# Stick-breaking attention from running products and differences of v, with every step of the stage in a list written out ahead

## The chip, the core and the metric

The kernel runs on one core of one Trainium2 chip. A core has five engines with an instruction queue each: TensorE (PE in the profile; its weight loads are the row PEld), VectorE (DVE), ScalarE (ACT), GpSimd (POOL) and SyncE (SP), which here issues nearly all DMAs. Each engine works through its queue in order, and an instruction that needs another engine's result waits for a semaphore. The metric is the device time of one execution in microseconds (us); the time before is 2201.22 us, the median of three runs from 2200.82 to 2202.71 us.

## The reference, cut to what matters

The model is a trunk of two layers over 1024 tokens of width 1024, in float32: an RG-LRU layer and a SwiGLU feed-forward layer, then an attention layer and a second feed-forward layer, and a last normalisation. Only the attention is concerned. It has 16 heads of 64 and is causal, and it has no softmax:

```
z = einsum("bhqd,bhkd->bhqk", qb, kb) * scale
strict = s_idx < t_idx
log_fail = where(strict, log_sigmoid(-z), 0.0)
suffix = cumsum(log_fail, axis=3, reverse=True) - log_fail
weights = where(strict, exp(log_sigmoid(z) + suffix), 0.0)
out = einsum("bhqk,bhkd->bhqd", weights, vb)
```

With F(r) = sigmoid(-z(r)), the weight of key s for query t is sigmoid(z(s)) times the product of F(r) over all keys r with s < r < t. Call R(s) the running product of F from key t-1 down to key s, with R(t) = 1. Then the weight is also R(s+1) - R(s).

## The kernel before

Matrix products are computed in three passes: each operand is split into a rounded high part and a low part (type fp32r), and `mm3` (lines 267 to 270) issues high by high, high by low and low by high, each with 128 rows, 128 columns of weights and up to 512 moving columns. All weights are loaded raw (`load_raw`, line 249), rounded on ACT and subtracted on DVE.

The attention stage lies between the first feed-forward layer and the second. Heads are taken in eight pairs, q = 0 to 7. For a pair, `qkv_steps` (from line 1523) projects q, k and v: three kinds times two halves n of the tokens are six groups of eight steps, a step being one `mm3`. A group's result is scaled by the norm on DVE (line 1544), split on ACT and DVE (1553, 1554) and moved by SP (1555) into tiles in which both halves of the 128 partitions hold what one head needs. The v projection is turned by four transposes on PE (1569) and split again (1573, 1574).

The scores of one head are cut into 12 chunks. A chunk is a block of 128 queries j against up to 512 keys: eight chunks end at the diagonal (128, 256, 384 and 512 keys, for j modulo 4), four more take the first 512 keys of the later blocks. A chunk is two products (`z_part`, 1596 and 1597), and a diagonal chunk of 128 keys is computed over 256. Then `z_rest` follows: F = sigmoid(-z) on ACT (1616), w = sigmoid(z) on ACT (1617), a running product of F from right to left on DVE (1620 at the diagonal, 1622 for the others, which start from the value that the diagonal chunk ended with), and w times the shifted product on POOL (1623). POOL also clears a column (1608) and ACT copies one (1612).

The weights must be turned to be multiplied with v. A unit takes a block kb of 128 keys against the four query blocks of a half G: up to four transposes on PE (1634), a split on ACT and DVE (1643, 1644) and two products with v (1655, 1656). A head has four units for the first half of the queries and eight for the second; a pair has 24. After a head's last unit of a half, ACT and DVE add up its two parts (1665, 1666), and after the second head of the pair the result is split: for most pairs it goes to DRAM (1675 to 1678) and is brought back later by `bring_back` (1505, 1506), for the last it is written in place (1671, 1672).

The order is a loop over units, u from -8 on: one chunk's products, the transposes of unit u + 2, the rest of the chunk, one item of a list of small things to do, two steps of the filling work, the products of unit u. The filling work is the projection of the pair after. The last pair has no pair after it; there the filling work is the output product's first two results, o = 0 and 1, over seven of the eight pairs of heads (14 steps). PE, DVE, ACT and POOL follow this order as it is written (`tc.manual_schedule(engines={E.PE, E.Activation, E.DVE, E.Pool})`). SP isn't in that list: the framework places its DMAs, and it puts loads ahead of what stands before them in the program.

Before the loop, 32 steps project q and k of pair 0. The weights of the next kind are asked for at the beginning of the present one, and their splits stand in the list `later`.

After the attention, `mix_out_ffn_in` (from line 713) computes the 16 results of the output product, o = 0 to 15, four for each pair of rows j: d in (j, j + 4) and the token halves n. A result is 24 products, is added to the residual h on DVE (877), and feeds `v_steps`, which prepares the operands of the feed-forward layer. The first two results, begun earlier, are completed there with six products for pair 7. The residual's 16 tiles are loaded by SP (369) into space that tiles of the attention held.

The recurrent layer has its order from a planner already: the class `Plan` takes tasks with an engine, a duration, what must end before, and a rank, and emits them in the order in which they could begin, ties going to the lower rank.

Of the kernel before, what the change touches and what calls it, by code (L numbers as in the profile page):

```python
# [34 lines left out]
class Plan:  # L35
# [7 lines left out]
    def emit(self):  # L43
        left, end, free, table = set(range(len(self.tasks))), {}, dict(self.free), {}
        while left:
            best = None
            for i in left:
                eng, us, _, after, rank, tab = self.tasks[i]
                after[:] = [a if isinstance(a, int) else a[0][a[1]] for a in after]
                if any(a not in end for a in after):  # L50
                    continue
# [11 lines left out]
            if eng == "dma":  # L63
                free[eng], end[i] = begin + 0.5, begin + us
            left.remove(i)
            fn()


def lru_plan(plan, order, fn):
# [101 lines left out]
    for k in range(3):  # L171
        weights(f"out{k}")


@with_exitstack
def trunk(
# [305 lines left out]
    with ExitStack() as st:  # L482
# [153 lines left out]
        class Steps:  # L636
            def __getitem__(self, key):
                return lambda: acts[key[0]](*key[1:])

        with tc.manual_schedule(engines={E.PE, E.Activation, E.DVE, E.Pool}):  # L640
# [4 lines left out]
                Steps(),  # L645
# [67 lines left out]
    def mix_out_ffn_in(h, mix, bias, layer, gnext, ob):  # L713
# [13 lines left out]
        if begun:  # L727
            ps_.enter_context(pos)
        else:
            po = ps_.enter_context(tc.tile_pool(name="fpo", bufs=1, space=PSUM, reuse_waits="tile"))  # L730
            ob = po.tile([P, S], F32, name="ob")
# [109 lines left out]
        procs = {3: 3, 4: 4, 6: 5, 8: 6, 10: 7}  # L841
        with tc.manual_schedule(engines={E.PE, E.Activation, E.DVE, E.Pool}):
# [12 lines left out]
            for j in range(HK):  # L855
                rows = (j, j + HK)
                dn = [(d, n) for d in rows for n in range(NH)] if j else [(d, n) for n in range(NH) for d in rows]
                for k, (d, n) in enumerate(dn):
                    o = HK * j + k
                    if begun and o < 2:  # L860
                        ps = half(ob, o)
                        for i in range(2 if o == 0 else 0):
                            hi, lo = mix.w[rows[i]]
                            mm3(half(ob, i), hi[:, ND - 1], lo[:, ND - 1], xh[ND - 1][0], xl[ND - 1][0], False, True)
# [37 lines left out]
                    if sq_todo:  # L902
                        squares(h, *sq_todo.pop(0), rbc[1:], acc)
                if j == HK - 1:
# [576 lines left out]
    pos = ExitStack()  # L1481
    with ExitStack() as st:
        ap = st.enter_context(tc.tile_pool(name="ap", bufs=1))
        qs, mix = ExitStack(), [Mix(attn_w_o, 0)]
        psZ = st.enter_context(tc.tile_pool(name="psZ", bufs=2, space=PSUM, reuse_waits="tile"))
        psT = st.enter_context(tc.tile_pool(name="psT", bufs=2, space=PSUM, reuse_waits="tile"))
        psO = st.enter_context(tc.tile_pool(name="psO", bufs=2, space=PSUM, reuse_waits="tile"))
# [324 lines left out]
```

## Time and profile before

| what | value |
|---|---|
| median of three runs | 2201.22 us |
| profiled execution, its own time | 2203.1 us |
| span of its trace | 2201.3 us, 28255 instructions |
| mean granted TensorE clock | 0.995 |
| busy share over the span | PE 99%, DVE 78%, ACT 52%, POOL 10% |

The trace runs from the first to the last instruction; some 1.8 us of the profiled execution's time lie around it. A group's row gives the line, the engine, the operation, what is written and read, the shapes and a count; then the time in which the group was busy, the mean duration of one in ns, and the idle time of the engine just before them with what ended it. Products overlap in the pipeline: the duration of one is longer than the distance from its start to the next one's start, so PE counts as busy also in short waits. A row by stretches gives the stretch, its length, each engine's busy time with the instructions in brackets, the granted clock, the share of the DMA engines and GB/s.

### The profile page before, as it was taken

The numbers are of one execution on the slowest core, as the hardware profiler recorded it, in microseconds if no ns is written. First come the engines' busy times: TensorE is split into PE (matmuls) and PEld (weight loads), VectorE is DVE, ScalarE is ACT, GpSimd is POOL, SyncE is SP. The second block draws the span as 40 slices with busy tenths as digits, with TensorE's granted clock in tenths as the row PEclk, the third lists the DMA queues.
The fourth block names the chain that finished last, engine by engine and source line by source line (L and its number), as shares of the span: only waits on it lengthen the run. The fifth ranks groups of instructions, "written<-read, shape, count | busy, mean of one in ns | idle before, by whom it ended". The sixth has DMA issues, their size and how long they took to land.

```text
span 2201.3 us, 28255 instructions
## 1 busy us (share of the span) xinstructions
PE 2169.1 (99%) x10054; PEld 1799.9 (82%) x10054; DVE 1726.9 (78%) x2413; ACT 1146.2 (52%) x2041; POOL 225.3 (10%) x356
## 2 busy tenths in 40 slices
PE   9999999999999999999999999999999999999997
PEld 7888888888888888878888888778888888888886
DVE  7978678677777887968888888866876777788886
ACT  5577444444444554646666666653534444454455
POOL 0000010000000000003333334422000000000001
PEclk9999999999999999999999999999999999999999
DMA  4111312344444864452333333731133444466442
GB/s 173 39 48 48 124 39 91 98 139 139 151 144 133 283 198 128 130 147 75 99 90 93 97 104 88 216 110 48 57 116 117 151 137 151 149 236 225 136 136 86
DMA packets 132316, 273.50 MB, mean 124 GB/s; under 512 B 15312, under 2 KB 22608, under 8 KB 132176
## 3 DMA queue, kind: packets, MB, share of 16 engines
q1 hardware_dynamic: 131744, 270.92, 38.9%
q8 instruction: 79, 1.29, 0.2%
q10 hardware_dynamic: 432, 0.79, 0.1%
q14 instruction: 61, 0.50, 0.1%
HBM read 175.70 MB, written 70.78 MB: 112 GB/s over the span
## 4 chain that ended last, share of the span: by engine, by line
PE 87%; DVE 8%; ACT 3%; issue 1%; DMA 1%; SPq 0%; DVEq 0%; POOL 0%; ACTq 0%; POOLq 0%
PE p_ps L270 18%; PE p_ps L268 18%; PE p_ps L269 18%; PE a_ps L268 3%; PE a_ps L269 3%; PE a_ps L270 3%; PE qk_ps L270 3%; PE qk_ps L268 3%; PE qk_ps L269 3%; PE ob_ps L268 2%; PE ob_ps L269 2%; PE ob_ps L270 2%; PE wt_ps L1634 2%; DVE F L1622 2%; PE z_ps L1597 1%
## 5 line engine op out<-in xcount | busy, mean ns | idle before, releaser
L1623 POOL TENSOR_TENSOR w<-w,F 128x128 f32<-128x128 f32 (+1 forms) x192 | 185.8, 968 | 311.5 <-DVE F L1620 173.2
L268 PE MATMUL p_ps<-vh,wbh 128*128 128x512 f32 x524 | 204.7, 391 | 2.0 <-ACT ta L1183 2.0
L270 PE MATMUL p_ps<-vh,wbl 128*128 128x512 f32 x524 | 204.8, 391 | 0.0
L270 PE MATMUL p_ps<-vh,wcl 128*128 128x512 f32 x524 | 204.1, 390 | 0.5 <-DVE wcl L802 0.5
L269 PE MATMUL p_ps<-vl,wbh 128*128 128x512 f32 x524 | 204.3, 390 | 0.0
L270 PE MATMUL p_ps<-vh,wal 128*128 128x512 f32 x524 | 204.1, 389 | 0.1
L268 PE MATMUL p_ps<-vh,wch 128*128 128x512 f32 x524 | 204.1, 389 | 0.0
L269 PE MATMUL p_ps<-vl,wch 128*128 128x512 f32 x524 | 203.9, 389 | 0.0
L269 PE MATMUL p_ps<-vl,wah 128*128 128x512 f32 x524 | 203.9, 389 | 0.0
L268 PE MATMUL p_ps<-vh,wah 128*128 128x512 f32 x524 | 203.8, 389 | 0.0
L788 ACT CAST wbh<-sb 128x1024 fp32r<-128x1024 f32 (+2 forms) x69 | 69.6, 1009 | 192.5 <-DVE sb L772 192.5
L1620 DVE TENSOR_TENSOR_SCAN F<-F,unit 128x128 f32<-128x128 f32 (+3 forms) x128 | 128.2, 1002 | 5.7 <-ACT F L1616 5.7
L1643 ACT CAST th<-wt_ps 128x512 fp32r<-128x512 f32 x192 | 93.4, 487 | 68.9 <-PE wt_ps L1634 67.0
L1644 DVE TENSOR_TENSOR tl<-wt_ps,th 128x512 fp32r<-128x512 f32 x192 | 104.8, 547 | 25.4 <-ACT th L1643 24.1
L268 PE MATMUL qk_ps<-vh,whi 128*128 128x512 f32 x264 | 118.8, 450 | 0.7 <-ACT vh L348 0.7
L268 PEld LDWEIGHTS p_ps<-vh,wbh 128*128 128x128 f32 x524 | 98.6, 188 | 22.6 <-ACT ta L1183 2.5
L270 PEld LDWEIGHTS p_ps<-vh,wbl 128*128 128x128 f32 x524 | 98.7, 188 | 21.9 <-DVE wbl L792 1.3
L270 PEld LDWEIGHTS p_ps<-vh,wcl 128*128 128x128 f32 x524 | 98.4, 188 | 21.8 <-DVE wcl L802 1.4
L270 PEld LDWEIGHTS p_ps<-vh,wal 128*128 128x128 f32 x524 | 98.4, 188 | 21.4 <-DVE wal L783 1.0
L269 PEld LDWEIGHTS p_ps<-vl,wbh 128*128 128x128 f32 x524 | 98.7, 188 | 20.4
L269 PEld LDWEIGHTS p_ps<-vl,wch 128*128 128x128 f32 x524 | 98.4, 188 | 20.3
L269 PEld LDWEIGHTS p_ps<-vl,wah 128*128 128x128 f32 x524 | 98.4, 188 | 20.3
(403 smaller groups left out, 5695.9 us busy)
## 6 DMA issues: line engine op xcount, KB each, us to landing
raw<-in_ffn_w_in SPq DMA_DIRECT2D x88, 512.0 KB, 3.6
vl<-pd SPq DMA_DIRECT2D x128, 256.0 KB, 3.6
pd<-U SPq DMA_DIRECT2D x90, 256.0 KB, 2.3
raw<-in_ffn_w_out SPq DMA_DIRECT2D x28, 512.0 KB, 4.1
raw<-in_attn_w_qkv SPq DMA_DIRECT2D x24, 512.0 KB, 3.5
acc<-pd SPq DMA_DIRECT2D x28, 256.0 KB, 2.7
pph<-rbc SPq DMA_DIRECT2D x28, 256.0 KB, 2.5
ppl<-acc SPq DMA_DIRECT2D x28, 256.0 KB, 2.6
```

Source lines behind the costliest of these rows:

```text
L268: nc.tensor.matmul(ps, lhsT=wh, rhs=mh, start=first, stop=False, **kw)
L269: nc.tensor.matmul(ps, lhsT=wh, rhs=ml, start=False, stop=False, **kw)
L270: nc.tensor.matmul(ps, lhsT=wl, rhs=mh, start=False, stop=last, **kw)
L788: nc.scalar.copy(self.full(self.wb), self.full(self.sb))
L1597: nc.tensor.matmul(ps[:, 0 : c1 - c0], lhsT=lhsT, rhs=KL[q][hx][:, c0:c1], start=False, stop=True)
L1620: nc.vector.tensor_tensor_scan(rev, rev, unit[:, NB - n :][:, ::-1], first, op0=ALU.mult, op1=ALU.add)
L1622: nc.vector.tensor_tensor_scan(rev, rev, rev, first, op0=ALU.mult, op1=ALU.bypass)
L1623: nc.gpsimd.tensor_mul(wt, wt, F[:, 1 : n + 1])
L1634: nc.tensor.transpose(tp[:, c : c + P], W[q, hx, j, kb // 4][:, (kb % 4) * P : (kb % 4 + 1) * P], ident)
L1643: nc.scalar.copy(th[:, q0:], tp[:, q0:])
L1644: nc.vector.tensor_sub(tl[:, q0:], tp[:, q0:], f32(th)[:, q0:])
```

## The change

**Running products.** With R from above, the sum over s < t of (R(s+1) - R(s)) v(s) equals v(t) plus the sum over s up to t of R(s) (v(s-1) - v(s)), with v(-1) = 0. So the running product itself is turned and multiplied, with differences of v in place of v. The second sigmoid (1617), the product on POOL (1623), the cleared and copied columns (1608, 1612) go. New are a difference of v on DVE for each half and pair (`v_diff`), ahead of the transposes, and an addition of v to the result (`v_add`), also once for each half and pair. A diagonal chunk of 128 keys is now computed over 128 columns.

**One planned order.** `attention_plan` (new) enters all steps of the stage in a `Plan`, with durations and ranks: projections, splits, moves, chunks, units, sums, loads. SP is in the list of engines whose order is fixed. The 32 steps for q and k of pair 0 stand before the plan, written out; there a kind's weights are loaded, in SP's order, behind the moves of the groups before it.

**The last pair.** The chunks and units of pair 7 go by halves of the queries: the first half for both heads, then the second half for both.

**Output products.** Four results are computed in the attention stage, each over all eight pairs of heads: o = 0 and 1 of the first rows, copied on ACT into the tiles `rbc`, and the first two of the second rows, left in PSUM. Their weights are loaded and split in the plan; those of the second rows are loaded and split once more for their other token half.

The planner's loop is rewritten to look only at tasks that are ready, and the distance of two DMAs in it is 0.55 instead of 0.5. The diff, cut to its core:

```
+    def weights(i, name, r, raw, use):
+        ld = plan.add("dma", 2.6, fn["load", name], [raw], r - 4)
+        h0 = plan.add("act", 0.5, fn["whi", name, 0], [ld, use], r - 2.5)
+        l0 = plan.add("dve", 0.6, fn["wlo", name, 0], [h0], r - 2.3)
...
+            for x in range(4 + 4 * which):
+                src = (tl if x % 2 else th) if which == 0 else (tl if x // 2 % 2 else th)
+                old = [(zlast, q - 2)] if q > 1 else []
+                m = plan.add("dma", 2.1, fn["move", q, which, n, x], [src, m, *old], s + 0.4)
...
+            dv[q, n] = plan.add("dve", 0.66, fn["dv", q, n], [pt[i], before, turned], s + 0.4)
+            if q == NP - 1:
+                m = None
+                for y in range(NP - 1 - n):
+                    for x in range(2):
+                        m = plan.add("dma", 2.4, fn["back", y, n, x], [p, (kept, (y, n)), m], s + 0.5)
...
+    for c, (q, hx, j, ci) in enumerate(chunks):
+        s, dg = c - LEAD, j // 4 == ci
+        need = [sig.get(c - 2), moved.get((q, 0, j // 4, hx)), moved.get((q, 1, ci, hx))]
+        zlast[q] = zz = plan.add("pe", 2 * mm(n), fn["z", c], need, s)
...
+    for u, (q, hx, G, kb) in enumerate(units):
+        if u in turns:
+            turn[v] = t = plan.add("pe", 0.45, fn["vt", *v, len(ring)], [dv[v], *ring[-2:-1]], u - 1.9)
...
+        need = [scan[q, hx, j, kb // 4] for j in js] + ring[-2:-1]
+        T[u] = plan.add("pe", 0.109 * len(js) + 0.02, fn["T", u, len(ring)], need, u - 1.8)
...
+        vadd[q, G] = plan.add("dve", 0.66, fn["vadd", q, G], [g1, pt.get(6 * q + 4 + G)], s + 0.5)
...
+    for o in range(4):
+        for k in range(ND):
+            need = [p, bank, wlo[f"o{o}"][k // 4], back[k, 0] if k < NP - 1 else kept[NP - 1, 0]]
+            p = plan.add("pe", 0.685, fn["ob", o, k], need, s + 4 * o + k / 2 + 0.6)
...
-        procs = {3: 3, 4: 4, 6: 5, 8: 6, 10: 7}
+        procs = {2: 3, 3: 4, 6: 5, 8: 6, 10: 7} if begun else {3: 3, 4: 4, 6: 5, 8: 6, 10: 7}
...
+                    if begun and o < 2:
+                        ps = rbc[o]
+                    elif begun and o in (HK, HK + 1):
+                        ps = early[o - HK]
...
-            nc.scalar.activation(F[:, 0:n], ps[:, 0:n], AF.Sigmoid, scale=-SC)
-            nc.scalar.activation(wt, ps[:, 0:n], AF.Sigmoid, scale=SC)
...
-            nc.gpsimd.tensor_mul(wt, wt, F[:, 1 : n + 1])
...
-        with tc.manual_schedule(engines={E.PE, E.Activation, E.DVE, E.Pool}):
+        with tc.manual_schedule(engines={E.PE, E.Activation, E.DVE, E.Pool, E.SP}):
+            sts, later = stats_steps(), []
+            for i in range(4 * ND):
...
+                g, k = divmod(i, ND)
+                if k == 0:
+                    if g:
+                        was = (0, (g - 1) // 2, (g - 1) % 2)
+                        scaled(*was)
+                        q_hi(*was)
+                        q_lo(*was)
+                        for x in range(4 + 4 * was[1]):
+                            move(*was, x)
+                    if g % 2 == 0:
+                        name = (0, g // 2 + 1)
+                        load(name)
+                        later += [
...
+               project(0, g // 2, g % 2, k)
+               if i >= 5 and later:
+                   later.pop(0)()
+            plan = Plan(pe=0.0, dve=1.0, act=1.0, dma=1.0)
+            chunks, units = attention_plan(plan, Steps(acts))
+            plan.emit()
+            mix.load(2)
```

More of the change, by code (lines that the diff above doesn't have):

```diff
@@ L63, in emit, with __init__, __getitem__ @@
             if eng == "dma":
-                free[eng], end[i] = begin + 0.5, begin + us
-            left.remove(i)
-            fn()
+                free[eng], end[i] = begin + 0.55, begin + us
+            ready.remove(i)
+            for y in users[i]:
+                todo[y] -= 1
+                if todo[y] == 0:
+                    ready.append(y)
+            fn()
+class Steps:
+    def __init__(self, acts):
+        self.acts = acts
+    def __getitem__(self, key):
+        return lambda: self.acts[key[0]](*key[1:])
 def lru_plan(plan, order, fn):
@@ L1492, in trunk @@
+        unit = own([P, NB], "unit")
         nc.gpsimd.memset(unit[:, 0 : NB - P], 0.0)
         nc.gpsimd.tensor_copy(unit[:, NB - P :], ident)
[L1494 to L1506 removed]
```

583 lines of the change are left out of this document (351 added, 232 removed).

## The prediction

> **What bounds the kernel now.** I read the first page, then busy time by stretches of the attention, then one pair, then single waits.
>
> ```profile
> span 2201.3 us, 28255 instructions
> ...
> PE 2169.1 (99%) x10054; PEld 1799.9 (82%) x10054; DVE 1726.9 (78%) x2413; ACT 1146.2 (52%) x2041; POOL 225.3 (10%) x356
> ...
> PE 87%; DVE 8%; ACT 3%; issue 1%; DMA 1%; SPq 0%; DVEq 0%; POOL 0%; ACTq 0%; POOLq 0%
> ```
>
> TensorE is busy nearly all the time and carries 87% of the chain that ended last. The change takes almost nothing from TensorE, so removed work on ACT, or all of POOL's 225.3 us, is worth nothing by itself. What can be won is TensorE's waiting. Where it waits in the attention, by stretches: the last of q and k of pair 0; seven pairs with filling work; the rest of pair 7; the output product. The last row is one pair.
>
> ```profile
> core 0: us, PE busy (x) PEld busy (x) DVE busy (x) ACT busy (x) POOL busy (x), PEclk, DMA share, GB/s
> 960.90:980.80 19.90, 19.90 (x97) 16.94 (x96) 8.33 (x17) 4.39 (x7) 0.00 (x0) 0.97 0.49 130
> 980.80:1421.40 440.60, 435.34 (x2315) 365.90 (x2314) 385.96 (x533) 289.48 (x721) 171.67 (x294) 1.00 0.38 103
> 1421.40:1468.00 46.60, 38.07 (x200) 30.95 (x199) 37.93 (x49) 29.87 (x73) 18.87 (x25) 0.93 0.30 108
> 1468.00:1544.20 76.20, 76.20 (x338) 63.09 (x337) 48.74 (x58) 27.86 (x43) 13.36 (x10) 1.00 0.29 97
> ```
>
> ```profile
> 1165.90:1226.80 60.90, 60.17 (x323) 50.56 (x322) 53.80 (x75) 40.22 (x102) 23.59 (x40) 1.00 0.35 96
> ```
>
> Idle of TensorE: none at the beginning, 440.60 - 435.34 = 5.3 us over the seven pairs (60.90 - 60.17 = 0.73 in one), 46.60 - 38.07 = 8.5 us in the last, where the granted clock is also 0.93: another 0.07 x 46.6 = 3.3 us. So 5.3 + 8.5 + 3.3 = 17 us is what better order could win at most by these rows.
>
> **Removed and added work.** Rows of the attention, by shape:
>
> ```profile
> L1622 DVE TENSOR_TENSOR_SCAN F<-F,F 128x512 f32<-128x512 f32 x64 | 96.0, 1501 | 4.9 <-ACT F L1616 1.9 <-POOL w L1623 1.7 <-issue 0.3
> L1620 DVE TENSOR_TENSOR_SCAN F<-F,unit 128x128 f32<-128x128 f32 x32 | 30.4, 950 | 4.9 <-ACT F L1616 4.9
> L1676 DVE TENSOR_TENSOR oo<-oo,oh 128x512 fp32r<-128x512 f32 x13 | 8.7, 666 | 0.0
> ```
>
> ```profile
> 982.62 0.42 DVE L1620 TENSOR_TENSOR_SCAN F<-F,unit 128x128 f32<-128x128 f32 x1 [4.94 <-ACT F L1616]
> ```
>
> ```profile
> 1423.83 1.28 DVE L1622 TENSOR_TENSOR_SCAN F<-F,F 128x512 f32<-128x512 f32 x1 [0.24 <-POOL w L1623]
> ```
>
> On DVE a pair gets two differences and two additions of v, at 0.666 us from line 1676 (same size, two inputs): 4 x 0.67 = +2.7 us. The first 128-key scan, while POOL was still waiting for it, took 0.42 us against a mean of 0.95; the 512-key one above took 1.28 against 1.50. With POOL gone I take the short values: 4 x 0.53 + 8 x 0.22 = -3.9 us a pair. DVE goes from 53.8 to about 52.6 us of 60.9 and stays second; TensorE hides it. If the scans kept their means, DVE would have 56.5 us and still fit: neither value moves the sum.
>
> The Trainium skill, "SBUF — State Buffer", section "SBUF: two separate sides", says that a VectorE instruction with two SBUF inputs and a GpSimd instruction that reads SBUF lock each other out for a whole instruction. The two rows of the 128-key scan agree. By that rule alone the change should win what DVE loses to the lock; by the stretch of one pair it wins nothing there, since TensorE ends last.
>
> The diagonal chunk of 128 keys goes from 256 to 128 columns on TensorE. Starts of products one after another:
>
> ```profile
> 1167.42 0.22 PE L1655 MATMUL av_ps<-th,v 128*128 128x128 f32 x1
> 1167.48 0.27 PE L1656 MATMUL av_ps<-tl,v 128*128 128x128 f32 x1
> 1167.60 0.33 PE L1596 MATMUL z_ps<-kh,q 128*128 128x256 f32 x1
> 1168.52 0.36 PE L1597 MATMUL z_ps<-kl,q 128*128 128x256 f32 x1 [0.59 <-DMA kl<-ql__9921]
> ...
> 1171.01 0.28 PE L1596 MATMUL z_ps<-kh,q 128*128 128x256 f32 x1
> 1171.12 0.28 PE L1597 MATMUL z_ps<-kl,q 128*128 128x256 f32 x1
> 1171.24 0.60 PE L1634 MATMUL wt_ps<-ident,w 128*128 128x128 f32 x4
> ```
>
> Two of 256 columns take 1171.24 - 1171.01 = 0.23 us, two of 128 take 1167.60 - 1167.42 = 0.18. Four such chunks in a pair and eight pairs: 32 x 0.05 = **-1.6 us**.
>
> **The order in the seven pairs.** In the fence above the score product waits 0.59 us for a move of k. That is most of the 0.73 of the pair. The plan gives each group's moves one after another 2.1 us apart before a chunk may follow, though SP issues them 0.6 us apart (below), so this wait should go. Bounds: if new waits of the same size arise, 0; if all goes, the 5.3 us and no more. I take nearly all: **-5.0 us**. Late next would be the turned differences of v, see the rivals.
>
> **The last pair.**
>
> ```profile
> 1426.62 1.11 PE L1569 MATMUL vt_ps<-ident,t 128*128 128x128 f32 x4 [2.92 <-DVE t L1544]
> ...
> 1429.83 0.77 PE L268 MATMUL ob<-vh,whi 128*128 128x512 f32 x1 [2.10 <-issue]
> 1430.40 0.63 PE L269 MATMUL ob<-vl,whi 128*128 128x512 f32 x1
> 1430.83 0.63 PE L270 MATMUL ob<-vh,wlo 128*128 128x512 f32 x1
> ```
>
> TensorE waits here for v's last half and for output weights, and after that products start 0.57 and 0.43 us apart, not the 76.20 / 338 = 0.225 of the output stretch. The change gives this stretch 96 output products instead of the 42 of its two times seven steps; 54 x 0.225 = 12.2 us move here from the output stretch, TensorE's sum unchanged. The work without losses is 46.6 - 8.5 - 3.3 = 34.8 us, with the moved products 47.0 us. DVE has 37.9 us here and gets three more weight splits (two pieces each of 0.67) and the additions, about 43 us: less than 47, so the products can cover its chain. Bounds of what is won: 0 (they stand too late in the list) and 11.8 us (no loss left). I take nearer the upper one, as the row puts the waits at single places and the new list has 54 more products to set there: **-9.3 us**, 2.5 us staying lost.
>
> The cover of the end shrinks. Between the last unit and the first product that needs its result stood 6 + 21 products (6.1 us), now 21 (4.7 us), and an addition of 0.67 us joins the chain:
>
> ```profile
> 1467.32 0.39 PE L1656 MATMUL av_ps<-tl,v 128*128 128x512 f32 x1
> ...
> 1468.36 0.69 DVE L1666 TENSOR_TENSOR oo<-av_ps,oo 64x512 f32<-64x512 f32 x1 [1.23 <-ACT oo L1665]
> 1469.74 0.69 DVE L1672 TENSOR_TENSOR vl<-oo,vh 128x512 fp32r<-128x512 f32 x1 [0.69 <-ACT vh L1671]
> ```
>
> From 1467.32, the start of the last unit's second product, to 1469.74 + 0.69 = 1470.43 are 3.1 us, with the addition 3.9: still under 4.7, cost 0. Without the cover it would be 3.9 us, once.
>
> **The start of the stage.** Here the change adds a wait. SP's order becomes the written one, and there the load of the raw v weights of pair 0 stands behind the moves of q's second half. Before, the framework had loaded ahead; the first row below is that load:
>
> ```profile
> 946.12 0.33 SPq L249 DMA_DIRECT2D raw<-in_attn_w_qkv  x1
> ...
> 971.62 1.13 SPq L1555 DMA_DIRECT2D q<-qh__7630  x2
> 972.80 2.30 SPq L1555 DMA_DIRECT2D q<-ql__7631  x2
> 975.20 0.53 SPq L249 DMA_DIRECT2D raw<-in_attn_w_qkv  x1
> ```
>
> ```profile
> 972.24 1.28 DVE L1511 TENSOR_TENSOR wlo<-raw,whi 128x512 fp32r<-128x512 f32 x2
> 975.57 0.69 DVE L1544 TENSOR_TENSOR t<-qk_ps,rbc 128x512 f32<-128x512 f32 x1 [2.04 <-PE qk_ps L270]
> 976.99 0.69 DVE L1554 TENSOR_TENSOR ql__7678<-t,qh__7677 128x512 fp32r<-128x512 f32 x1 [0.73 <-ACT qh__7677 L1553]
> ```
>
> ```profile
> raw<-in_attn_w_qkv SPq DMA_DIRECT2D x24, 512.0 KB, 3.5
> ```
>
> ```profile
> 981.85 0.36 PE L1597 MATMUL z_ps<-kl,q 128*128 128x256 f32 x1 [0.76 <-DMA kl<-ql__7678]
> ```
>
> With the load at 975.2 instead of 946.12 the raw tile lands at 975.2 + 3.5 = 978.7; the split's first rounding takes about 0.65 on ACT, the two subtractions on DVE 1.28: 980.6. Behind them in DVE's queue stands the scaling of k's first half, which started at 975.57. It, the split, the moves and the score product shift by 980.6 - 975.57 = 5.0 us, to 986.9; the score product waits already, so all of it falls on TensorE, because the plan's first chunk has a lower rank (-8) than the v projection's first step (-7.5). Behind the wait come slow products as at 1429.83, about 1 us. **+6.0 us.** Bounds: 0, if the load is hoisted after all, and 5.0 + 3.3, if the clock costs what it cost in the last pair.
>
> The Trainium skill, "TensorE: Matmul & The Clock Gate", Part 1, says that the clock halves after an idle window of about 3.4 us and needs as long a busy one to return; the intervals after 1429.83 agree. By the page such a wait costs up to 1.7 us more, an estimate from 3.4 x 0.5, and the sum would be 0.7 us longer.
>
> Moved with no cost: output weights are loaded twice for two rows (2 loads, 4 roundings, 4 subtractions), hidden by the 47 us stretch. The planner's 0.55 doesn't reorder the recurrent layer, whose loads each wait for the one before.
>
> **The sum.** -1.6 - 5.0 - 9.3 + 6.0 = -9.9 us. The profiled execution took 2203.1 us (span 2201.3), which gives 2193.2; it stands 1.9 us above the median, so on the median's scale 2201.2 - 9.9 = **2191 us**.
>
> **Rivals.** *No wait at the start*: the load is placed early; 2191 - 6 = 2185. For it: the first recurrent stage fixed SP's order too, and TensorE has 99%. Against it: the diff writes the load behind the moves.
>
> *The last pair's gain stays out*: the plan sets the returns of stored results 2.4 us apart in a chain, so the products that need them stand late in TensorE's list, and the waits before them remain. 2191 + 9.3 = 2200. For it: up to 14 returns in the chain make 33 us of the 47. Against it: two results begin with the first return.
>
> *Behind the residual's loads.* SP issues them when tiles come free, and later weights stand behind them:
>
> ```profile
> 1467.75 7.84 SPq L369 DMA_DIRECT2D hh<-hd  x14
> 1475.96 0.33 SPq L249 DMA_DIRECT2D raw<-in_attn_w_o  x1
> ```
>
> If the fourth pair of weights now comes behind 16 loads (16/14 x 8.2 = 9.4 us, landing 3.5, splits 1.05 + 1.28) and these wait for the last addition (3.9), it is ready after 19 us; the products before it last 3 x 24 x 0.225 = 16.2. Cost about 3 us: 2194.
>
> *Slower: the turned differences of v.* They stand in the ring of transposes, and behind each stands every later unit. Their chain has one more DVE step than before, and in the fence of the last pair the old chain kept TensorE for 2.92 us. There are 14 turns under filling work. At 2.92 each the time is 2191 + 41 = 2232; from (2205.6 - 2191) / 14 = 1.05 us a turn on, the kernel is slower. Against it: the mean pair has only 0.73 us of waiting for two turns.
>
> **How the numbers follow.** My forecast 0.38 (2187 to 2196, its terms' middle values); no wait at the start 0.17; last pair's gain out 0.15; behind the residual's loads 0.10; slower by late turns, or by other waits that a fixed order adds, 0.20. 0.2% is 4.4 us, about what a measurement of this kernel can tell from no change. Faster by over that is below 2196.8: forecast, start and residual, 0.65. The last pair's 2200 is "same", 0.15. Slower 0.20. The lower end is 2177: no wait at the start and all 17 us won, taken 1.37 times, as the wait at 1168.52 cost 0.92 - 0.11 = 0.81 us where its row shows 0.59, since TensorE's overlap hides the rest: 2201.2 - 1.6 - 23. The upper end, 2208, is the slower case at 1.2 us a turn; beyond it lies about half of that case.
>
> **What would show it.** Right: DVE 40-odd of 47 us and TensorE over 44 of 47 in the last pair; an idle of some 5 us before the first score product with "DMA kl" as releaser; pairs of about 60 us; an output stretch of 64 us. Wrong: no such idle, or a pair longer than 61 us with waits on line 1569's successor or on transposes.

## The result, and the profile after

The changed kernel takes 2201.14 us (median of 12 runs, 2199.77 to 2202.80) where the kernel before, run beside it, takes 2202.68 us (12 runs, 2200.82 to 2206.23): a ratio of 0.9992, 95% interval 0.9984 to 1.0001. No difference can be told. The profiled execution took 2201.81 us, its span is 2200.0.

The first page of the changed kernel: busy time by engine, and the chain that ended last.

```profile
span 2200.0 us, 27262 instructions
...
PE 2167.9 (99%) x10054; PEld 1798.9 (82%) x10054; DVE 1709.1 (78%) x2434; ACT 1078.5 (49%) x1776; POOL 35.6 (2%) x44
...
PE 90%; DVE 5%; ACT 2%; DMA 2%; issue 1%; SPq 0%; DVEq 0%; ACTq 0%
```

993 instructions, 190 us of POOL's work and 68 us of ACT's are gone; TensorE's busy time differs by 1.2 us. DMA has gone from 1% of the chain to 2%. Medians here are of all executions, ratios and intervals of the fast ones alone: one of the six of moves_close was slow (2458.92 us, granted clock 0.831).

Busy time by stretches of the changed kernel: the seven pairs, the last pair, the output product.

```profile
core 0: us, PE busy (x) PEld busy (x) DVE busy (x) ACT busy (x) POOL busy (x), PEclk, DMA share, GB/s
988.30:1430.60 442.30, 434.60 (x2313) 365.64 (x2314) 366.66 (x548) 228.03 (x479) 0.59 (x6) 1.00 0.38 103
1430.60:1478.00 47.40, 46.15 (x248) 37.88 (x248) 35.37 (x53) 23.51 (x49) 0.00 (x0) 1.00 0.51 187
1478.00:1543.30 65.30, 65.30 (x289) 54.05 (x288) 51.35 (x59) 27.88 (x43) 13.63 (x10) 1.00 0.25 85
```

The last pair and the output product came out in size as forecast: 48 products more stand in the last pair, its stretch is as long as before, and the output stretch is 10.9 us shorter. The seven pairs still have 442.30 - 434.60 = 7.7 us without TensorE.

To compare kernels, the attention is cut below by four starts of products in each trace: the first product of q's projection, the 145th of the projections (before it lie the 144 products for q, k and v of pair 0, and the first chunks), the last of the projections, and the first of the output stretch, up to the first product of the feed-forward layer. What follows that lasts 655.6 to 657.9 us in every kernel. Start stretches of equal code differ by up to 4 us between traces; no reading of the start below hangs on less.

| kernel | start | seven pairs | last pair | output | median us |
|---|---|---|---|---|---|
| before | 47.3 | 423.6 | 46.9 | 76.2 | 2202.7 |
| after | 55.1 | 425.3 | 47.3 | 65.3 | 2201.1 |
| load_early | 47.3 | 427.3 | 47.2 | 65.3 | 2196.5 |
| moves_together | 54.3 | 418.3 | 47.3 | 65.3 | 2193.3 |
| moves_close | 56.3 | 420.5 | 47.2 | 65.3 | 2196.8 |
| both_edits | 45.0 | 417.5 | 47.3 | 65.3 | 2185.1 |
| load_on_pool | 45.1 | 418.7 | 47.3 | 65.3 | 2185.8 |
| both_and_pool_load | 45.0 | 417.8 | 47.3 | 65.3 | 2184.4 |
| pool_back | 52.1 | 438.4 | 48.2 | 65.3 | 2215.6 |
| both_pool | 47.6 | 424.5 | 48.3 | 65.3 | 2194.1 |
| two_results | 52.6 | 425.1 | 38.1 | 76.2 | 2203.7 |
| by_heads | 53.9 | 427.2 | 56.0 | 65.3 | 2210.8 |
| heads_two_results | 53.1 | 427.0 | 45.0 | 76.2 | 2211.8 |
| before_sp_fixed | 58.2 | 512.4 | 47.1 | 76.2 | 2302.8 |

The change won 10.4 us at the end (last pair and output), lost 7.8 at the start, and lost 1.7 in the seven pairs, where a gain of 6.6 had been forecast.

What TensorE waits for in the attention of the changed kernel (total, times, longest):

```profile
PE z_ps L1786 <- DMA kl<-ql: 8.3, 8, 1.6
PE z_ps L1786 <- DMA kh<-qh: 4.4, 1, 4.4
```

Nearly all of it is moves of k. The 4.4 us, and 0.62 of the 8.3, stand at the start. SP's, DVE's and TensorE's timelines there:

```profile
975.11 1.72 SPq L1746 DMA_DIRECT2D q<-ql  x1
976.87 0.58 SPq L425 DMA_DIRECT2D raw<-in_attn_w_qkv  x1
```

```profile
981.23 1.29 DVE L1701 TENSOR_TENSOR wlo<-raw,whi 128x512 fp32r<-128x512 f32 x2 [7.29 <-ACT whi L1697]
982.44 0.68 DVE L1723 TENSOR_TENSOR t<-qk_ps,rbc 128x512 f32<-128x512 f32 x1
```

```profile
987.01 0.44 PE L1786 MATMUL z_ps<-kh,q 128*128 128x128 f32 x1 [4.38 <-DMA kh<-qh]
988.07 0.44 PE L1786 MATMUL z_ps<-kl,q 128*128 128x128 f32 x1 [0.62 <-DMA kl<-ql]
988.31 0.74 PE L444 MATMUL qk_ps<-vh,whi 128*128 128x512 f32 x1
988.85 0.63 PE L445 MATMUL qk_ps<-vl,whi 128*128 128x512 f32 x1
989.28 0.63 PE L446 MATMUL qk_ps<-vh,wlo 128*128 128x512 f32 x1
```

This is the chain of the forecast: SP issued the raw load of v's weights at 976.87, behind the last move of q; its split on DVE ran from 981.23, and the scaling of k's first half started behind it, at 982.44. TensorE's wait is 4.38 + 0.62 = 5.0 us, and the products behind it start 0.54 and 0.43 us apart. By the view of stretches the granted clock (third number from the end) is 0.50 there:

```profile
988.30:991.50 3.20, 3.20 (x10) 2.63 (x11) 1.12 (x2) 0.79 (x2) 0.00 (x0) 0.50 0.82 185
```

The rest of the 8.3 us comes mostly once in each pair, at the 128-key chunk of the upper keys. One pair's wait on TensorE, and SP's timeline ahead of it:

```profile
1179.43 0.30 PE L1786 MATMUL z_ps<-kl,q 128*128 128x128 f32 x1 [1.09 <-DMA kl<-ql]
```

```profile
1172.36 1.11 SPq L1746 DMA_DIRECT2D kl<-ql  x2
1174.66 0.34 SPq L425 DMA_DIRECT2D raw<-in_attn_w_qkv  x1
1175.05 0.46 SPq L1746 DMA_DIRECT2D kl<-ql  x1
```

Three moves of k stand in the trace from 1172 to 1176, the last of them 0.39 us behind a 512 KB load. The time from issue to landing of these three (least, median, most):

```profile
DMA to landing us min/median/max: 2.5/2.5/4.3
```

The two ahead of the load land after 2.5 us. The one behind it takes 4.25: issued at 1175.05, landed at 1179.30, and the product that waits for it starts at 1179.43. The load itself was held in SP's list from 1173.52 to 1174.66, until DVE's split had freed its tile, and the moves behind it were held with it. Six pairs have this wait, 1.0 to 1.6 us long, and in the trace all six have the same picture: the move that ends the wait was issued 0.4 us behind a 512 KB load and landed after 4.2 to 4.8 us.

### The profile page after: what moved, and what is told of

The parts are those of the page before. It is cut to its first block, busy times and chain, and to the rows that moved or that the text cites. A ratio compares the mean times of both kernels' runs of the same rounds, so it can differ in the third digit from the quotient of the medians.

```text
span 2200.0 us, 27262 instructions
## 1 busy us (share of the span) xinstructions
PE 2167.9 (99%) x10054; PEld 1798.9 (82%) x10054; DVE 1709.1 (78%) x2434; ACT 1078.5 (49%) x1776; POOL 35.6 (2%) x44
## 4 chain that ended last, share of the span: by engine, by line
PE 90%; DVE 5%; ACT 2%; DMA 2%; issue 1%; SPq 0%; DVEq 0%; ACTq 0%
PE p_ps L446 18%; PE p_ps L444 18%; PE p_ps L445 18%; PE qk_ps L444 3%; PE qk_ps L445 3%; PE qk_ps L446 3%; PE z_ps L1786 3%; PE a_ps L445 3%; PE a_ps L444 3%; PE a_ps L446 3%; PE av_ps L1834 3%; PE wt_ps L1817 2%; PE ob_ps L444 2%; PE ob_ps L445 2%; PE ob_ps L446 2%; DMA kl<-ql 2%
## 5 line engine op out<-in xcount | busy, mean ns | idle before, releaser
L1798 ACT ACTIVATE F<-z_ps 128x512 f32<-128x512 f32 (+3 forms) x188 | 91.8, 490 | 168.3 <-PE z_ps L1786 167.2
L1805 DVE TENSOR_TENSOR_SCAN F<-F,unit 128x128 f32<-128x128 f32 (+3 forms) x128 | 104.8, 821 | 62.9 <-ACT F L1798 62.7
L444 PEld LDWEIGHTS p_ps<-vh,wah 128*128 128x128 f32 x524 | 98.4, 188 | 20.3
L444 PEld LDWEIGHTS p_ps<-vh,wch 128*128 128x128 f32 x524 | 98.4, 188 | 20.3
```

Of the source, the lines that this page charges most:

```text
L444: nc.tensor.matmul(ps, lhsT=wh, rhs=mh, start=first, stop=False, **kw)
L1798: nc.scalar.activation(F, Z.pop(c)[:, 0:n], AF.Sigmoid, scale=-SC)
L1805: V.tensor_tensor_scan(rev, rev, unit[:, NB - n :][:, ::-1], 0.0, op0=ALU.mult, op1=ALU.add)
```

## The experiments

My theory after this profile: two separate losses, both made by the new order of SP's list, eat the gain at the end. One is the load at the start, the other the place of the loads among the moves in the pairs. The rivals are with each run. Ratios are to the kernel before, run on the same chip.

**The start: the loads issued earlier (load_early).** Both raw loads that pair 0 still needs are issued with the first group.

```
                     if g % 2 == 0:
                         name = (0, g // 2 + 1)
-                        load(name)
...
+                    if g == 0:
+                        load((0, 1))
+                        load((0, 2))
```

> One edit on the changed kernel: the raw v weights of pair 0 are loaded beside those of k, at the first of the 32 written-out steps, ahead of all moves. Theory: the gap before the first score product (4.4 us in front of it and 0.6 us between its two halves, then slow products) is the late load alone; both waits shrink to under 1 us, and the time falls by 5.0 to 7.8 us, to about 2194 us. Rival (the gap comes from the written order of SP as a whole, or from the split and the moves of k, not from this load): the gap stays above 3 us and the time within 2 us of 2201.

2196.45 us, ratio 0.9970 (0.9958 to 0.9982): 4.7 us less than the changed kernel, a little short of the theory's 5.0 to 7.8. The start is 47.3 us again, as before the change: 7.8 us less. The first score product no longer waits for k. In the seven pairs 2.0 us more were lost; the waits on kl stay, 9.1 us. So the start's loss is the place of the load, and the pairs' loss is another one.

**The pairs: moves that don't hang on each other (moves_together, moves_close).** In the plan each move hung on the one before. The dependence is taken out; the time from a move to the chunk that needs it is set to 6.0 in one kernel and left at 2.1 in the other.

```
-                m = plan.add("dma", 2.1, fn["move", q, which, n, x], [src, m, *old], s + 0.4)
+                m = plan.add("dma", 6.0, fn["move", q, which, n, x], [src, *old], s + 0.4)
```

> One edit on the changed kernel: in the plan a move of q or k no longer follows the end of the move before it, and a move counts 6.0 us, so that the chunks stay about as late in TensorE's list as they are. The eight moves of a group then stand together in SP's list. Theory (loads, stores and the other half's moves stand between a group's moves and hold up the last one): TensorE's waits for kl, 8.3 us in all, fall under 2 us, and the time to about 2193 us (2191 to 2196). Rival (k's projection, scaling and split come late themselves): the waits stay, 2201 us.

> As the run with the moves together, but a move still counts 2.1 us in the plan, so that the first chunks of a pair stand some 4 us earlier in TensorE's list. Theory: the moves are together too, but a chunk may follow them so closely that four moves of 0.6 us and a landing of 2.3 us (4.7 us against 3.8 planned) are not done; half the gain, 2194 to 2200 us. Rival (order in TensorE's list does not matter): the same time as with 6.0 us.

With 6.0: 2193.29 us, ratio 0.9953 (0.9941 to 0.9965). With 2.1: 2196.77 us, 0.9965 (0.9953 to 0.9978). The seven pairs fall from 425.3 to 418.3 and 420.5 us. SP's list around the same pair with 6.0, and TensorE's waits on moves in the whole attention:

```profile
1166.94 1.29 SPq L1746 DMA_DIRECT2D kl<-ql  x2
1168.28 0.59 SPq L1746 DMA_DIRECT2D kh<-qh  x1
1168.91 1.24 SPq L1746 DMA_DIRECT2D kl<-ql  x2
1170.25 0.54 SPq L1895 DMA_DIRECT2D odh<-oh  x1
1171.21 0.33 SPq L425 DMA_DIRECT2D raw<-in_attn_w_qkv  x1
```

```profile
PE z_ps L1786 <- DMA kh<-qh: 4.7, 1, 4.7
PE z_ps L1786 <- DMA kl<-ql: 0.6, 1, 0.6
```

All the moves of the group now stand ahead of the store and the load. The waits on kl go from 8.3 to 0.6 us, and the 0.6 stands at the start; the 4.7 us ahead of the first score product stay, as that load wasn't touched. With 2.1, 5.3 us of waits on kl were left, in three waits, the longest 4.1. By the trace all three stand between 987 and 999 us, so they belong to the start; in the seven pairs no wait on a move is left with 2.1 either. The time lies in the forecast 2194 to 2200, but not for the reason given: no chunk of the pairs came too early for its moves. What the pairs lose against 6.0, 420.5 - 418.3 = 2.2 us, is in good part one wait near their end for v's split on DVE, 2.6 us instead of 1.5. What cured the pairs is that the moves no longer hang on each other; the planned time from move to chunk mattered little.

**Both (both_edits).**

> Both earlier edits in one kernel: the raw loads of the second and third kind of pair 0 are issued with the first group, and the plan's moves no longer hang on the move before. My theory (two separate losses, one at the start and one in the pairs): the gains add. The start's edit alone gave 0.30% against the kernel before and the moves' edit alone 0.47%, of which the last pair is common to both; beside the changed kernel (2201.1) they were 4.7 and 7.9 us, so 2201.1 - 12.6 = about 2188.5 us, ratio 0.993, no idle of over 2 us ahead of the first score product and under 1 us of waits on moves of k in all pairs. Rival (one loss seen in two places: whoever takes the first away finds the second later in the list): no better than the moves' edit alone, 2193, ratio 0.995 or more.

2185.11 us, ratio 0.9918 (0.9905 to 0.9932). The losses are separate: 0.22% and 0.39% against the changed kernel alone, 0.74% together, 0.13 more than their sum, about what one interval leaves open to either side. Start, pairs and end are now 45.0, 417.5 and 112.6 us against 47.3, 423.6 and 123.0 before.

**Is it the load in SP's list? (load_on_pool).** The same loads, at the same place in the program, are issued by POOL. Nothing else is changed.

```
-                raws[name] = load_raw(w_qkv[name[1] * ND + name[0]])
+                raws[name] = rp.tile([P, D], F32, tag="raw", name="raw")
+                nc.gpsimd.dma_start(raws[name], w_qkv[name[1] * ND + name[0]])
```

> The changed kernel with the 512 KB loads of the weights of q, k and v in the attention issued by POOL, which has almost nothing else to do there, instead of SP; their place in the written order stays. Theory (in SP's list the load waits for the tile's last reader and is then issued ahead of moves of k; the moves behind it are late for the wait and for the transfer ahead of them): the idle ahead of the first score product goes from 4.4 to under 1 us, as the load no longer stands behind the moves of q, and the waits on kl from 8.3 to under 3; 2201.1 - 4.7 - 6 = about 2190, ratio 0.994 to 0.996. Rival 1 (the transfers share the DMA engines whoever issues them): the start's idle goes, the waits on kl stay above 5 us, 2196. Rival 2 (issuing on POOL is slow, or the loads wait there for each other): new waits on weights, 2201 or more.

2185.81 us, ratio 0.9924 (0.9912 to 0.9936): this one edit brings what the two edits bring, 4 us more than I had expected. Start 45.1, pairs 418.7, waits on kl 1.5 us. In the same pair SP's and POOL's lists read:

```profile
1159.92 1.74 SPq L1747 DMA_DIRECT2D kl<-ql  x3
1161.70 1.24 SPq L1747 DMA_DIRECT2D kh<-qh  x2
1162.98 1.24 SPq L1747 DMA_DIRECT2D kl<-ql  x2
```

```profile
1162.81 0.54 POOL L1690 DMA_DIRECT2D raw<-in_attn_w_qkv  x1 [22.29 <-ACT th L1823]
```

POOL's queue, not SP's, now waits for the tile, and SP's moves go out without a pause. The moves of kl issued from 1158.6 to 1161.1 landed after 2.4 to 2.8 us. The move at 1162.98, 0.17 us behind POOL's load, took 4.9:

```profile
DMA to landing us min/median/max: 4.9/4.9/4.9
```

So rival 1 has a part of the truth: a 512 KB load slows the moves behind it, whichever queue issues it. No chunk was waiting for these. What cost time was that the load stood ahead of the urgent ones.

> Both edits together, and the attention's loads of weights of q, k and v issued by POOL. Theory (the remaining waits of the stage are not from SP's list: 0.2 us on moves of k were left): within 2 us of both edits alone, 2183 to 2187. Rival (the loads in SP's list still delay results' stores and moves that the profile's single waits don't show): 3 us or more faster, 2182 and below.

Both edits and the load on POOL: 2184.38 us, ratio 0.9916 (0.9902 to 0.9929), the fastest version run and within the error of both_edits. The remaining waits are not from SP's list.

**The order of SP alone, on the kernel before (before_sp_fixed).**

```
-        with tc.manual_schedule(engines={E.PE, E.Activation, E.DVE, E.Pool}):
+        with tc.manual_schedule(engines={E.PE, E.Activation, E.DVE, E.Pool, E.SP}):
```

> One edit on the kernel before: SP is added to the engines whose order is as written, nothing else. Theory: the raw v weights of pair 0 come behind q's moves as in the changed kernel, the first score product waits some 5 us more, and the kernel is 5 to 8 us slower than before (2207 to 2210 us); the pairs keep their period of 60.9 us, since in the written order a group's moves stand together. Rival (the fixed list costs nothing by itself): 2202 us.

2302.79 us, ratio 1.0448 (1.0435 to 1.0462). All expectations missed by far. Waits of TensorE, then of ACT (from 1000 to 1500 us):

```profile
PE z_ps L1596 <- ACT w L1617: 63.5, 25, 6.4
```

```profile
ACT whi L1510 <- DMA raw<-in_attn_w_qkv: 83.9, 13, 8.7
```

What the start lost on one load is lost here on many. In the order as it is written the raw loads stand behind moves, which wait for results; the rounding of the raw tile then stops ACT's queue, behind it wait the sigmoids of the chunks, and for these TensorE. In the kernel before, ACT has no such wait among its six largest from 1000 to 1420 us. The 63.5 us are not the whole loss of 100; the mean granted clock is also lower, 0.981. A fixed order of SP costs 100 us here as the program was written. The changed kernel's list costs some 16 us against the one of both_edits (2201.1 against 2185.1), which is fixed too: what costs is the order, not that it is fixed.

**POOL's work back (pool_back, both_pool).** For each chunk POOL multiplies the running products by themselves into a scratch tile, as dead work; first on the changed kernel, then on both_edits.

```
+            wd = own([P, 256], "wd", BF16)
+            for a in range(0, n, 256):
+                b = min(n, a + 256)
+                F = F_[q, hx, j, ci][:, a:b]
+                nc.gpsimd.tensor_mul(wd[:, 0 : b - a], F, F)
```

> The changed kernel with POOL's work beside the scans put back as dead work: for each chunk POOL multiplies the running products by themselves into a scratch tile of bf16 that nobody reads. Theory (the scans' time is worth nothing, as TensorE ends last): the 128-key scans go from 0.42 us back towards 0.95 and those of 512 keys from 1.22 to about 1.5, DVE's busy time rises by some 30 to 45 us, and the time stays within 3 us of the changed kernel's 2201. Rival (the change's gain in the pairs hangs on the scans without POOL beside them, and other losses ate it): 5 us or more slower, 2206 and up, with new waits of TensorE on transposes of the weights in the pairs.

2215.55 us, ratio 1.0060 (1.0046 to 1.0073): 14 us slower than the changed kernel, so the theory fell. But the rival's place was wrong too. Waits of TensorE from 960 to 1560 us:

```profile
PE z_ps L1786 <- DMA kl<-ql: 14.1, 7, 2.4
PE z_ps L1786 <- DMA kh<-qh: 3.7, 1, 3.7
PE vt_ps L1757 <- DVE dv L1751: 1.5, 3, 0.8
```

The waits on moves of k went from 8.3 to 14.1 us. In the pair shown above DVE's split frees the raw tile later: SP's load is held for 1.8 us instead of 1.1, the moves behind it come later, and the wait is 2.0 us instead of 1.09. So a slower DVE reached TensorE through SP's list. But that is at most 5.8 of the 13.1 us by which the seven pairs are longer (438.4 against 425.3). The dead product also does more than lengthen scans: it reads F, and ACT has to wait for it before it writes that tile again (waits of ACT from 990 to 1430 us; the changed kernel has none on POOL):

```profile
ACT F L1798 <- POOL wd L1812: 34.7, 25, 1.8
```

How much of the rest comes that way stays open.

> Both edits as in the earlier kernel that had them together, and POOL's dead product beside the scans put back. Theory (POOL's work costs only where a late VectorE step makes SP's load, and with it the moves behind it, late): with moves that do not hang on each other the same dead work costs little: 2185.1 + 0 to 4 = 2185 to 2189, waits on kl under 2 us. Rival (longer scans reach TensorE by another way, the weights' transposes or the turned differences of v): the same 13 to 15 us as on the changed kernel, 2198 to 2200.

2194.09 us, ratio 0.9958 (0.9944 to 0.9971): 9 us slower than both_edits, between theory and rival. With moves that no longer hang on the loads the waits on k are gone, and the next thing is late (waits from 990 to 1423 us):

```profile
PE vt_ps L1757 <- DVE dv L1751: 5.2, 9, 1.1
```

These are the turned differences of v. Seven of the nine waits, 4.0 of the 5.2 us by the trace, stand behind a difference that had itself waited for POOL, which clears the column ahead of v in its own queue, behind the dead products:

```profile
DVE dv L1751 <- POOL vt L1721: 3.0, 7, 0.9
```

In both_edits DVE never waits for POOL there. So the 9 us are not the price of longer scans alone, and these two runs don't say what the removal of POOL's work was worth in the change: they show that as much work on POOL, put there, costs 9 to 14 us. Scans by shape, both_pool and then both_edits:

```profile
L1807 DVE TENSOR_TENSOR_SCAN F<-F,F 128x512 f32<-128x512 f32 x56 | 78.6, 1403 | 9.2 <-ACT F L1798 9.0
...
L1805 DVE TENSOR_TENSOR_SCAN F<-F,unit 128x128 f32<-128x128 f32 x30 | 14.9, 495 | 0.2 <-ACT F L1798 0.2
```

```profile
L1807 DVE TENSOR_TENSOR_SCAN F<-F,F 128x512 f32<-128x512 f32 x56 | 71.6, 1279 | 12.3 <-ACT F L1798 11.9
...
L1805 DVE TENSOR_TENSOR_SCAN F<-F,unit 128x128 f32<-128x128 f32 x31 | 12.8, 414 | 0.2 <-ACT F L1798 0.2
```

The dead product adds some 0.1 us to the mean scan, less than the scans of the kernel before had lost (mean 0.95 for 128 keys). It isn't spread evenly: of the scans of 128 keys about half keep 0.41 to 0.42 us and the longest takes 0.63, of those of 512 keys 34 of 56 keep 1.26 to 1.30 and the longest takes 1.73. It is not the same product: it writes bf16 and starts at another moment. The Trainium skill, "SBUF — State Buffer", section "SBUF: two separate sides", has a VectorE instruction with two SBUF inputs and a GpSimd one that reads SBUF locking each other out for a whole instruction. Longer scans beside POOL agree in direction; whether a scan that grew waited for the rest of one POOL product (mean 0.51 us for 128 columns, 0.75 for 256) no run here separates.

**Halves or heads, four results or two (two_results, by_heads, heads_two_results).** What carried the gain at the end? Two results instead of four move 48 products back to the output stretch; the other edit takes pair 7 head by head, like the other pairs.

```
-    for o in range(4):
+    for o in range(2):
...
-    mix_ffn(1, h, mix, None, None, [OB[2], OB[3]])
+    mix_ffn(1, h, mix, None, None, [])
```

```
-        if q < NP - 1:
+        if True:
             for h in heads:
                 chunks += diag(h, range(NT)) + rest(h)
                 units += lower(h) + upper(h)
```

> The changed kernel with two instead of four output results begun in the last pair: 48 of its 96 products go back to the output stretch. Theory (the last pair's products only filled idle time that was there): the last pair's stretch stays near 47 us, though its TensorE work falls by 48 x 0.225 = 10.8 us to about 36, and the output stretch grows from 65.3 to 76; the whole is 9 to 11 us slower than the changed kernel, 2210 to 2212, ratio to the kernel before about 1.003. Rival (halves instead of heads made the last pair shorter by themselves, the products hardly matter): the last pair's stretch falls with the work, towards 38 to 40 us, and the whole is within 3 us of 2201.

> The changed kernel with its last pair in the order of the other seven, head after head instead of half after half; the output products between and everything else stay. Theory (the products of the first half of the rows need the last pair only for their last step, and 21 of 24 products of each result are independent of the order): under 3 us slower, as the first half's result of the last unit comes later but products of other results stand between; 2201 to 2204. Rival (the halves carry the gain of the last pair): 5 us slower or more, with TensorE idle ahead of the first output product that reads the last pair's result.

> The changed kernel with its last pair in the order of the other seven and only two output results begun in it: the fourth cell of the table halves or heads, four or two results. From the last product of a q, k, v projection to the first of the feed-forward the other three took 112.7 us (halves, four), 114.3 (halves, two) and 121.3 (heads, four). Theory (the order by halves carries the gain, 8.7 us, the 48 further products 1.6): about 123 us here, like the 123.0 of the kernel before, in all some 2212 us. Rival (heads lose only because four results' products then come late in one block, and two do not): about 115 us, 2204.

Last pair and output together, from the table above:

| | four results | two results |
|---|---|---|
| by halves | 112.7 us | 114.3 us |
| by heads | 121.3 us | 121.2 us |

The totals are 2203.66 us (1.0003, 0.9994 to 1.0012) for halves with two, 2210.84 (1.0036, 1.0023 to 1.0048) for heads with four, 2211.75 (1.0038, 1.0024 to 1.0051) for heads with two. The order by halves is worth 7 to 9 us, the two further results 1.6 us at most. My theory for two_results was wrong: the stretch of the last pair shrank with its work, to 38.1 us. So was that for by_heads, under 3 us slower: it is 9.7. By heads, four results don't help; the stretches of its trace show where the time goes:

```profile
1460.00:1464.00 4.00, 1.99 (x13) 1.27 (x11) 4.00 (x6) 2.18 (x5) 0.00 (x0) 1.00 0.00 0
1464.00:1468.00 4.00, 1.75 (x7) 0.83 (x7) 3.90 (x7) 1.50 (x4) 0.00 (x0) 0.82 0.00 0
1468.00:1472.90 4.90, 4.78 (x17) 4.20 (x18) 2.35 (x5) 2.02 (x4) 0.00 (x0) 0.50 0.48 121
1472.90:1478.00 5.10, 5.10 (x24) 4.29 (x23) 0.00 (x0) 0.59 (x1) 0.00 (x0) 0.95 0.94 335
```

From 1460 to 1468 TensorE works half the time while DVE (fourth pair of numbers) is full: the last head's scans and splits come one after another, with no product between. The products stand behind, from 1470.2 to 1484.3 nearly all in one block. The same place of the changed kernel, by halves:

```profile
1456.00:1460.00 4.00, 4.00 (x20) 3.29 (x19) 4.00 (x5) 1.17 (x2) 0.00 (x0) 1.00 0.00 0
```

DVE is as full, but the block of output products stands here, from 1454.97 to 1464.5, and some more between the last units. The plan gives a reason, which I haven't tested by itself: results 2 and 3 wait for the banks of 0 and 1, and these are complete only with pair 7's first half. By halves that is a third of the pair's units, by heads two thirds. It can't be the whole reason: heads_two_results has no results 2 and 3 there, loses as much, and shows the same gap:

```profile
1460.00:1464.00 4.00, 1.91 (x14) 1.59 (x15) 4.00 (x7) 1.79 (x4) 0.00 (x0) 1.00 0.00 0
1464.00:1468.00 4.00, 2.30 (x11) 1.38 (x10) 3.87 (x7) 1.26 (x3) 0.00 (x0) 0.69 0.00 0
```

## Why the prediction was right or wrong

It was wrong: 2191 us and a clear gain were forecast, and none was measured. 2201.14 lies in its range, in the case "same", but for another reason than the one given for that case: the last pair's gain came. By the table the sum is -10.4 (end) + 7.8 (start) + 1.7 (pairs, the diagonal chunk with them) = -0.9 instead of -9.9, and 8.3 of the 9 us between lie in the pairs.

- **The start of the stage, +6.0.** Right in its chain, a little small in its size. The load was issued at 976.87, not 975.2, and the score product of the low part came at 988.07, not 986.9: 6.2 us late instead of 5.0. The slow products cost 1.3 where 1 was taken: six took 990.99 - 988.31 = 2.7 us (the next score product started at 990.99), six at 0.23 take 1.4. At the 145th projection product 7.8 us are lost in all (kernels with the same start differ by up to 4 us there), inside the upper bound of 8.3. The estimate worked out from the Trainium skill, "TensorE: Matmul & The Clock Gate", Part 1, was up to 1.7 us for it; 1.3 in these six products agrees.
- **The order in the seven pairs, -5.0.** This step failed. It said that the wait for a move of k should go, as the plan sets the moves 2.1 us apart and SP issues them 0.6 apart. SP does issue them so, but the planned distance is what the order is made from: between two moves of one group it set the other group's moves, a store and a raw load, and SP then works this list as it stands. The wait per pair grew from 0.59 to 1.09 us in the pair shown and to 1.6 at most. The bound "0, if new waits of the same size arise" was too mild: the pairs got 1.7 us longer. Of the signs named, a pair longer than 61 us did come (the waits at 1179.43 and 1240.86 lie 61.4 us apart), but its wait was for a move of k, not for a transpose. With the chain cut, the pairs of both_edits take 6.1 us less than before, against 6.6 forecast with the term for the columns.
- **Removed and added work.** The scans came down as forecast, to 0.41 us for 128 keys and 1.28 for 512 (rows of both_edits above), and DVE's work in a pair to 50.8 us (52.6 forecast; last row of this point). That POOL's work is "worth nothing by itself" holds no more in the new order: a like amount of it costs 14 us there, and 9 when the moves are mended, in part by ways of its own (tiles it holds, a clearing that comes late behind it). TensorE's full row hid short waits that are set by what DVE and POOL finish late (some 0.5 us each in both_pool, 2.0 to 2.4 in pool_back).

```profile
1118.60:1179.50 60.90, 59.81 (x321) 50.31 (x321) 50.82 (x76) 31.52 (x66) 0.10 (x1) 1.00 0.35 95
```

- **The diagonal chunk, -1.6.** Not tested by a run of its own. In the trace of both_edits, from the start of its first product to that of the product behind its second, a chunk takes 0.17 us with 128 columns and 0.23 with 256 (medians of 28 each): 32 x 0.06 = 1.9 us, so the term stands.
- **The last pair, -9.3.** The size was right, 10.4 us measured, TensorE busy 46.15 of 47.40 us. The reason was wrong, so that the size came out is luck. I gave it to 54 products that cover DVE's chain; the order by halves carries it, and I had given that no term. DVE's work in the stretch is 35.4 us, not 43.
- **The cover of the end, 0, and the residual's loads.** Right: TensorE is busy in 65.30 of 65.30 us of the output stretch, and its 288 output products take 0.227 us each, as the 336 before did, so neither the shorter cover nor the 16 loads cost anything. This answers that rival.
- **No wait at the start.** It was put at 2185, and did not occur. load_early, which makes it so, gives 2196.5; 2185 needed the pairs as well (both_edits, load_on_pool).
- **Slower by turned differences of v.** No such wait among those of the changed kernel. It can come: in both_pool it costs 5.2 us in nine waits, seven of them behind a difference that waited for POOL. The clause "or by other waits that a fixed order adds" names what happened, without its place.

What I could have done: where a change gives a queue a fixed order, write that queue's list down for one pair, with the waits of each entry and what stands behind it. I did so for the start, and there the forecast holds; for the pairs I read durations from the plan and not the order that follows from them.

## What to carry to other kernels

A queue that issues DMAs in order is an engine like the others: an entry that waits for a free tile holds back every transfer behind it, and a big transfer makes the small ones behind it late (here 512 KB ahead of 128 KB, some 2 us). Put urgent small moves ahead of bulk loads, or give the loads to a queue that has nothing urgent; and in a planner, don't use a dependence to express a distance in time, since the planner fills the gap with other entries. A helper engine's work may look free by the busy rows and still cost: follow the short waits of the bound engine back to what sets them, and when work is put back as a test, see which tiles and queues it holds besides.

## What the runs showed of the hardware that I had not expected

- A 128 KB move issued 0.2 to 0.4 us behind a 512 KB load lands after 4.2 to 4.9 us instead of 2.3 to 2.8, in the same queue (1175.05 in the changed kernel) and also when the load is in another (1162.98 in load_on_pool).
- The granted clock falls without a long idle time. In by_heads no single wait from 1455 to 1470 is over 1.1 us, TensorE is busy 1.99 and then 1.75 of 4 us, and the clock goes to 0.82 and then 0.50 for 4.9 us, in which the output products start 0.43 us apart.
